# One group of probability transposes, retention scores and value products on TensorE, and a deeper split-ahead for twelve steps

## The chip, the cores and the metric

The kernel runs on one core of one Trainium2 chip. The metric is the time of one execution on the device in microseconds (us), taken as the median of several runs. A difference of under about 0.2% can't be told from no change by this measurement.

## What is computed

One transformer block on 256 tokens of width 1024: a modulation from a conditioning vector, a token mixer with two heads of different kinds (block attention and retention), and a convolutional feed-forward part, each with a layer norm behind it. What matters here is the middle of the mixer. With 256 tokens the attention has a single block, so it is plain causal attention over 8 heads of width 64:

```python
l_own = jnp.einsum('bhqd,bhkd->bhqk', qc, k_own).astype(jnp.float32) * scale
l_own = jnp.where(causal, l_own, NEG_BIG)
...
p = jax.nn.softmax(logits, axis=-1).astype(v.dtype)
...
return (jnp.einsum('bhqk,bhkd->bhqd', p_own, v_own)
...
```

and the retention has 4 heads of key width 128 and value width 256:

```python
scores = jnp.einsum('bhncd,bhnkd->bhnck', qc, kc) * d_intra[None, :, None].astype(dt)
intra = jnp.einsum('bhnck,bhnkv->bhncv', scores, vc)
...
y_r = head_norm(y_r).transpose(0, 2, 1, 3).reshape(b, s, RET_V_W)
y_r = jax.nn.silu(rg) * y_r
merged = jax.nn.sigmoid(g_a) * (y_a @ w_proj_moba) + jax.nn.sigmoid(g_r) * (y_r @ w_proj_ret)
```

The kernel does not scan over chunks: it takes the whole 256 x 256 causal score matrix of a retention head at once and multiplies it by a table of decays.

## The kernel before

**The main stream.** All large products run as *steps*. A weight matrix comes from HBM in raw tiles of 128 x 2048 (1 MB), each of which holds two *halves* of 128 x 1024. A half is split into two fp32r tiles: ScalarE (ACT) copies it to `whi` (L1338) and VectorE (DVE) subtracts that from the raw half to get `wlo` (L1352). A step then multiplies one half on TensorE (PE) with three products, high by high, high by low and low by high (L123 to L125). In the region of this change a step is 12 matmuls of 128x512. There are 4 raw buffers and 8 pairs of split tiles.

**What runs when.** The list `steps` is walked in order. Steps 0 to 7 make the retention's queries and keys, 8 to 11 the second half of its values, 12 to 19 its gate (`winB`, a Silu), 20 to 23 one sigmoid gate (`winGa`), 24 to 31 the other (`winGr`). Products of 12 to 15 go to PSUM banks 2 and 3, of 16 to 19 to 0 and 1, of 20 and 21 to 2 and 3, of 22 and 23 to 0 and 1, and 24 begins with 2 and 3 again. DVE empties the banks of the `winGa` steps (L539) and ACT those of the gate before (L531). In front of each step `prep_to` splits halves ahead: in the range of this change 5 halves beyond that of the step (`NEAR`), as long as fewer than 8 split halves are live. With each half that is split, DVE also gets one product and sum of another part, the modulation (`ada`, L255), as long as such a raw tile is loaded.

**Side work.** Attention and retention are Python generators, advanced at three points of each step: A ahead of the splitting, B behind it, and C behind the step's matmuls. What they issue at C stands on PE behind the matmuls of this step. Every engine takes its own instructions in the order in which they are written. Attention's loop `for i in range(HM + 5)` runs at step 6 + i: its softmax pieces are on ACT at B (L1156, L1160), the reciprocal on DVE at C (L1164). The probabilities of a head, 256 x 256 without the part above the diagonal, are transposed on PE in three blocks of 128x128 into a PSUM bank (L1171) and copied to SBUF by ACT (L1173). That happens behind step 10 for heads 0 and 1, behind step 14 for heads 2 to 5 and behind step 16 for 6 and 7. Behind step 18 stand the attention's value products (`attend`, L1147) and then the retention's scores (L1231), which DVE multiplies by the decay (L1234). Behind step 19 stand the retention's value products (L1219 to L1221), copied out by ACT to `yr` (L1223). All these are plain fp32 matmuls, while the steps are fp32r. The transposes and L1219 to L1221 use the whole array of 128 x 128, L1125 and L1231 two halves of 64 rows, L1147 two halves of 64 columns; so the profile prints 128*128, 64*128 and 128*64.

Of the kernel before, what the change touches and what calls it, by code (L numbers as in the profile page):

```python
# [9 lines left out]
AF = mybir.ActivationFunctionType  # L10
OP = mybir.AluOpType

T, D = 256, 1024
HM, DM = 8, 64
HR, DK, DV = 4, 128, 256
# [2 lines left out]
EPS = 1e-5  # L18
ALPHA = 2.0 ** 0.25
RROPE, RET_AT, TL = 2, 10, 4  # L20
LOOKAHEAD, NEAR, NEAR_TO = 6, 5, 47
RAW_BUFS = 4
HL_BUFS = 8
NG = 4
# [44 lines left out]
def _body(nc, a, out, pe, act, dve, sp, cst, wts, big, tmp, ps, dram):  # L69
    f = lambda ap: ap.bitcast(F32)  # L70

    def bank(i):
        return ps.tile([128, 512], F32, tag=f"P{i}", name=f"P{i}")
# [1017 lines left out]
    def mixers():  # L1091


        qk = S["qk"]
        qkT = [slot(n, [128, 4, 256]) for n in ("3a", "3b")]
        roped = lambda i: rope(qk[i], consts["cosm"][:, i], consts["sinm"][:, i])
        roped(0)
        for i in range(ROT_AT + 2):
            yield
            if i == 1:  # L1100
                roped(1)
            yield
# [12 lines left out]
        blk = [slice(128 * qb, 128 + 256 * qb) for qb in range(2)]  # L1115

        def scores(h):


            S["sc"] = [bank(b) for b in ((4, 7, 5, 6), (2, 3, 4, 7))[h // 4]]  # L1120
            for w in range(2):
                for qb, c in enumerate(blk):
                    for e in range(2):
                        s = slice(64 * e, 64 * e + 64)
                        pe.matmul(S["sc"][2 * w + e][:, c], qkT[0][s, h // 2 + w, qb * 128:(qb + 1) * 128],  # L1125
                                  qkT[1][s, h // 2 + w, :128 + 128 * qb], start=True, stop=True)

        def maxima(h):

            for e in range(2):  # L1130
                sm = S["sms"][:, (h + e) % (TL + 2)]
                mx = tmp.tile([128, 8], F32, name="mx", bufs=TL + 2)
                for qb, c in enumerate(blk):
                    dve.tensor_tensor_reduce(out=sm[:, c], in0=S["sc"][h % 4 + e][:, c],
                                             in1=consts["mask"][:, 128 - 128 * qb:],
                                             scale=-0.125, scalar=3.0e38, op0=OP.add, op1=OP.min,
                                             accum_out=mx[:, 2 + qb:3 + qb])
                st[h + e] = sm, mx

        def attend(h, p):  # L1140

            for w in range(2):
                pT = [pt.pop(h + 2 * w + e) for e in range(2)]
                for kb, (o, c) in enumerate(((slice(0, 256), slice(0, 256)), (slice(128, 256), slice(256, 384)))):
                    for e in range(2):
                        u = h + 2 * w + e
                        pe.matmul(p[64 * e:64 * e + 64, 256 * w + o.start:256 * w + o.stop],  # L1147
                                  v[:, kb, 64 * u:64 * u + 64], pT[e][:, c], start=kb == 0, stop=kb == 1)
            return lambda: split(yah[:, h // 2:h // 2 + 2], yal[:, h // 2:h // 2 + 2], p.rearrange("p (w t) -> p w t", w=2))

        for i in range(HM + 5):
            yield
            if 0 <= i - 2 < HM:
                sm, mx = st[i - 2]
                for qb, c in enumerate(blk):
                    act.activation(sm[:, c], sm[:, c], AF.Copy, scale=mx[:, 6 + qb:7 + qb])  # L1156
            if 0 <= i - 1 < HM:
                sm, mx = st[i - 1]
                for qb, c in enumerate(blk):
                    act.activation(sm[:, c], sm[:, c], AF.Exp, scale=-1.0, bias=mx[:, 2 + qb:3 + qb],  # L1160
                                   accum_out=mx[:, 4 + qb:5 + qb])
            yield
            if 0 <= i - 1 < HM:
                dve.reciprocal(mx[:, 6:8], mx[:, 4:6])  # L1164
            if i == HM + 4:
                done = [attend(4 * g, bank(5 + g)) for g in range(2)]
            for h in {4: (0, 1), 8: (2, 3, 4, 5), 10: (6, 7)}.get(i, ()):
                sm, mx = st.pop(h)
                p = bank(h - 2 if h in (2, 3) else 5 + h % 2)
                for b in range(3):  # L1170
                    pe.transpose(p[:, b * 128:(b + 1) * 128], sm[:, b * 128:(b + 1) * 128], ident)  # L1171
                pT = sm if h > 1 else slot(("9a", "9b")[h], [128, 384])
                act.activation(pT, p[:, :384], AF.Copy)  # L1173
                pt[h] = pT
            if i == 0:
                S["sms"] = slot(11, [128, TL + 2, 384])
            if i in (0, 4):
                scores(i)
            if i in (0, 2, 4, 5):
                maxima(i + i % 2)  # L1180
            if i == RROPE:
                S["turn"] = [rotate(n) for n in range(2)]
            if i >= RROPE and S["turn"] and next(S["turn"][0], 1) == 1:
                S["turn"].pop(0)
            if i == RET_AT:
                sides.append(retention())
            yield
        for fn in done:
            fn()

    def retention():
        rot, decay, sms = S["rot"], S["decay"], S["sms"]
        while S["main"] < RV_AT:
            yield
            yield
            yield
        rv = S["rv"]
        yr = [slot(n, [128, 1024]) for n in ("8a", "8b")]
        SCORES, VALUES = ((4, 7), (2, 3)), (5, 6, 4, 7)
        stt = tmp.tile([128, 8, 6], F32, name="stt", bufs=1)  # L1200
        mv = tmp.tile([128, 8, 2], F32, name="mvr", bufs=1)
        sd = tmp.tile([128, 8], F32, name="sdr", bufs=1)
        ds_ = {}
        for _ in range(3):
            yield
        for n in range(4):
            yield
            if n > 1:
                for t in range(4):
                    g = 2 * n - 4 + t // 2  # L1210
                    dve.bn_stats(stt[:, 2 * g + t % 2], yr[t % 2][:, g * 256:(g + 1) * 256])
                    dve.bn_aggr(mv[:, 2 * g + t % 2], stt[:, 2 * g + t % 2:2 * g + t % 2 + 1])
            yield
            if n == 1:
                for g in range(HR):
                    d_ = ds_.pop(g)
                    p = bank(VALUES[g])
                    c = slice(g * 256, (g + 1) * 256)
                    pe.matmul(p[:, 0:256], d_[:, 0:128], rv[0][:, c], start=True, stop=True)  # L1219
                    pe.matmul(p[:, 256:512], d_[:, 128:256], rv[0][:, c], start=True, stop=False)  # L1220
                    pe.matmul(p[:, 256:512], d_[:, 256:384], rv[1][:, c], start=False, stop=True)  # L1221
                    for t in range(2):
                        act.activation(yr[t][:, c], p[:, t * 256:(t + 1) * 256], AF.Copy)  # L1223
            for m in range(HR // 2 * (n == 0)):
                pp = [bank(b) for b in SCORES[m]]
                for o, ks, qs in ((slice(0, 256), slice(0, 128), slice(0, 256)),
                                  (slice(256, 384), slice(128, 256), slice(128, 256))):
                    for i in range(2):
                        for e, p in enumerate(pp):
                            r_ = slice(64 * e, 64 * e + 64)  # L1230
                            pe.matmul(p[:, o], rot[m][r_, 2 + i, ks], rot[m][r_, i, qs], start=i == 0, stop=i == 1)  # L1231
                for h, p in zip((2 * m, 2 * m + 1), pp):
                    d_ = sms[:, (HM + h) % (TL + 2)]
                    dve.tensor_tensor(d_, p[:, :384], decay[h // 2][:, h % 2], OP.mult)  # L1234
                    ds_[h] = d_
            yield
        S["x"] = [slot(n, [128, 1024]) for n in ("2a", "2b")]
        for i in range(2):
# [148 lines left out]
    for s, (need, rel, fn) in enumerate(steps):  # L1387
        S["main"] = s
        if s == LN1_AT + 8:
            sides.append(residual())  # L1390
        run_sides()
        prep_to(max(need) + 1, True)
        late = LN1_AT < s < LN1_AT + 8
        if not late:
            prep_to(max(need) + 1 + (NEAR if s < NEAR_TO else LOOKAHEAD if s < LN1_AT - 1 else HL_BUFS))
        run_sides()
        for e in waiting:
            if e[0] <= s:
# [120 lines left out]
```

## Time and profile before

| | |
|---|---|
| median of 3 runs | 421.67 us (421.6 to 421.73) |
| the profiled execution's own time | 421.43 us |
| its span in the profile | 419.7 us |
| granted TensorE clock, mean | 0.997 |
| DVE busy from 110 to 118 us | 8.00 of 8.00 us |
| ACT busy from 110 to 118 us | 7.97 of 8.00 us |
| ACT busy from 118 to 124 us | 2.95 of 6.00 us |
| PE busy from 107 to 138 us | 31.00 of 31.00 us |

A page of the profile gives, for one execution, the busy time of each engine, the chain of work that ended last, and the largest groups of instructions. The trace behind it answers closer questions: a timeline by engine, the chain in order of time, who waited for whom. The difference of 1.7 us between own time and span lies around the profiled instructions. Matmuls are pipelined, so the durations of neighbours overlap; the distance from one start to the next tells what one costs.

### The profile page before, as it was taken

To read this page: it belongs to the slowest core of one execution; us is meant where nothing else is said; L and a number is where in the kernel's file an instruction comes from. 1 tells how busy PE (TensorE), PEld (TensorE's weight loads), DVE (VectorE), ACT (ScalarE), POOL (GpSimd) and SP (SyncE) were. 2 spreads that over 40 slices of the span, in tenths; PEclk is the share of its full clock that TensorE was granted. 3 is DMA by queue.
4 is the path that set the end of the run, shared out by engine and by line. 5 is a ranking of instruction groups with operands and counts; after the bars stand their busy time and mean duration, and the time that the engine had idled before them with its cause. 6 is when DMAs were issued, how large, how long until landed. Compare 5 with 4: busy or idle time off the path is not lost.

```text
span 419.7 us, 5879 instructions
## 1 busy us (share of the span) xinstructions
PE 412.5 (98%) x2140; PEld 348.1 (83%) x2140; DVE 368.1 (88%) x597; ACT 248.5 (59%) x410; POOL 14.0 (3%) x26
## 2 busy tenths in 40 slices
PE   7999999999999999999999999999999999999995
PEld 4888888888878888888888898888888888888884
DVE  6889799969998889899887987999999888789996
ACT  5666568787955587535544886555555545455700
POOL 0000000100001000001000001000000010003200
PEclk9999999999999999999999999999999999999998
DMA  8998997685688768789662094985866777450002
GB/s 298 405 410 328 414 404 302 247 324 208 222 308 328 254 244 346 304 319 341 223 269 101 1 361 169 373 295 189 307 260 215 281 284 242 187 198 2 1 6 97
DMA packets 18541, 105.60 MB, mean 252 GB/s; under 512 B 2256, under 2 KB 3536, under 8 KB 7760
## 3 DMA queue, kind: packets, MB, share of 16 engines
q1 hardware_dynamic: 16992, 99.70, 63.1%
q0 software_dynamic: 1376, 4.99, 3.5%
q10 hardware_dynamic: 144, 0.52, 0.5%
q8 instruction: 17, 0.28, 0.3%
q14 instruction: 12, 0.10, 0.1%
HBM read 104.15 MB, written 1.06 MB: 251 GB/s over the span
## 4 chain that ended last, share of the span: by engine, by line
PE 97%; DVE 1%; DMA 1%; issue 0%; DVEq 0%; ACT 0%; ACTq 0%
PE P L134 19%; PE P L123 15%; PE P L124 15%; PE P L125 15%; PE P L329 13%; PE P L138 10%; DMA raw<-in_m 1%; PE P L731 1%; PE P L734 1%; PE P L733 1%; PE P L1125 1%; PE P L1231 1%; PE P L1147 1%; PE P L1171 1%; DVE unread L266 1%; PE P L675 0%
## 5 line engine op out<-in xcount | busy, mean ns | idle before, releaser
L1352 DVE TENSOR_TENSOR wlo<-raw,whi 128x1024 fp32r<-128x1024 f32 x118 | 141.9, 1220 | 14.0 <-ACT whi L1338 13.8
L1338 ACT ACTIVATE whi<-raw 128x1024 fp32r<-128x1024 f32 x118 | 122.1, 1056 | 39.3 <-DMA raw<-in_wpr 10.6
L123 PE MATMUL P<-whi,AH 128*128 128x512 f32 x128 | 50.6, 395 | 0.0
L125 PE MATMUL P<-whi,AH 128*128 128x512 f32 x128 | 49.9, 390 | 0.0
L124 PE MATMUL P<-wlo,AH 128*128 128x512 f32 x128 | 49.8, 389 | 0.0
L329 PE MATMUL P<-whi,AH 128*128 128x512 f32 x160 | 41.7, 391 | 1.1 <-DVE AH L295 1.1
L134 PE MATMUL P<-AYa,whi 128*128 128x512 f32 x144 | 41.7, 391 | 0.0
L255 DVE CUSTOM_DVE_ANT_0 junk<-raw,srow 128x1024 bf16<-128x1024 f32 x32 | 39.0, 1219 | 0.0
L134 PE MATMUL P<-AYb,whi 128*128 128x512 f32 x144 | 38.7, 390 | 0.0
L329 PEld LDWEIGHTS P<-whi,AH 128*128 128x128 f32 x160 | 29.8, 188 | 8.4 <-ACT whi L312 1.9
L489 ACT ACTIVATE A<-P 128x256 f32<-128x256 f32 x36 | 13.7, 381 | 33.9 <-PE P L138 23.6
L134 PEld LDWEIGHTS P<-AYb,whi 128*128 128x128 f32 x144 | 27.0, 188 | 6.0
L312 ACT ACTIVATE whi<-raw 128x512 fp32r<-128x512 f32 (+1 forms) x26 | 20.8, 824 | 17.7 <-DMA raw<-in_b 16.3
L134 PEld LDWEIGHTS P<-AYa,whi 128*128 128x128 f32 x144 | 25.8, 189 | 4.2
L315 DVE TENSOR_TENSOR wlo<-raw,whi 128x512 fp32r<-128x512 f32 (+1 forms) x26 | 23.5, 936 | 6.2 <-ACT whi L312 5.8
L123 PEld LDWEIGHTS P<-whi,AH 128*128 128x128 f32 x128 | 24.0, 188 | 5.2 <-issue 0.3
L125 PEld LDWEIGHTS P<-whi,AH 128*128 128x128 f32 x128 | 24.0, 188 | 5.1
L124 PEld LDWEIGHTS P<-wlo,AH 128*128 128x128 f32 x128 | 24.1, 188 | 4.8
L329 PE MATMUL P<-wlo,AH 128*128 128x512 f32 x80 | 23.2, 390 | 0.0
L138 PE MATMUL P<-AYb,wlo 128*128 128x256 f32 x144 | 23.1, 283 | 0.0
L138 PE MATMUL P<-AYa,wlo 128*128 128x256 f32 x144 | 23.0, 282 | 0.0
L138 PEld LDWEIGHTS P<-AYa,wlo 128*128 128x128 f32 x144 | 20.9, 190 | 1.4
(323 smaller groups left out, 776.1 us busy)
## 6 DMA issues: line engine op xcount, KB each, us to landing
raw<-in_ada SPq DMA_DIRECT2D x16, 1024.0 KB, 5.1
raw<-in_wup SPq DMA_DIRECT2D x11, 1024.0 KB, 5.7
raw<-in_wgate SPq DMA_DIRECT2D x11, 1024.0 KB, 5.7
raw<-in_wdown SPq DMA_DIRECT2D x11, 1024.0 KB, 4.9
raw<-in_winB SPq DMA_DIRECT2D x6, 1024.0 KB, 6.8
raw<-in_m SPq DMA_DIRECT2D x4, 1024.0 KB, 8.3
raw<-in_b SPq DMA_DIRECT2D x4, 1024.0 KB, 7.2
raw<-in_wrot SPq DMA_DIRECT2D x4, 1024.0 KB, 7.4
```

The costliest lines, as they stand in the source:

```text
L123: pe.matmul(o, lh, rh, start=start, stop=False)
L124: pe.matmul(o, lh, rl, start=False, stop=False)
L125: pe.matmul(o, ll, rh, start=False, stop=stop)
L134: pe.matmul(banks()[half], t[0][:, k * 128:(k + 1) * 128], x2(k), start=k == 0, stop=half > 0 and k == 7)
L138: pe.matmul(banks()[half][:, :256], t[1][:, k * 128:(k + 1) * 128], x2(k)[:, 0], start=False, stop=half == 0 and k == 7)
L255: dve.tensor_tensor_reduce(out=nobody(j if own else None), in0=raw, in1=srow, scale=1.0, scalar=0.0, op0=OP.mult, op1=OP.add, accum_out=mo ...
L312: act.activation(hi[:, o], raw[:, o], AF.Copy)
L315: dve.tensor_tensor(lo[:, o], raw[:, o], f(hi[:, o]), OP.subtract)
L329: pe.matmul(pa[b0 + c // 512 * 2 + t], x[xi][:, j, t * 128:(t + 1) * 128], ws[k][:, c:c + 512], start=first and (xi, k) == (0, 0), stop=la ...
L489: act.activation(t, p[:, 256:], AF.Copy)
L1338: act.activation(hi, src, AF.Copy)
L1352: dve.tensor_tensor(lo, src, f(hi), OP.subtract)
```

## The change

The groups of fp32 work behind steps 14, 16, 18 and 19 become one group behind step 17. In it stand, in this order: the transposes of heads 2 to 7, the retention's scores and their decay products, three halves more of splitting (`S["ahead"]`), the attention's value products, the retention's value products and their copies. The decay products are written in place into the decay tile, no longer into the tile of the probabilities. The banks of the group are dealt anew. The splits of the attention's output (`done`) go from the beginning of step 19 to step 18 behind its splitting, and the retention's statistics one step forward. For steps 18 to 29 the splitting is asked to run 8 halves ahead where it ran 5; since a half counts as live until its step is done, that keeps 7 beyond the one in use. The transposes of heads 0 and 1 stay behind step 10.

```diff
-LOOKAHEAD, NEAR, NEAR_TO = 6, 5, 47
+LOOKAHEAD, NEAR, NEAR_TO, WIDE = 6, 5, 47, range(18, 30)
...
+        def turned(hs):
+
+            for h in hs:
+                sm, mx = st.pop(h)
+                p = bank((5, 6, 2, 3, 4, 7, 5, 6)[h])
+                for b in range(3):
+                    pe.transpose(p[:, b * 128:(b + 1) * 128], sm[:, b * 128:(b + 1) * 128], ident)
+                pT = sm if h > 1 else slot(("9a", "9b")[h], [128, 384])
+                act.activation(pT, p[:, :384], AF.Copy)
+                pt[h] = pT
...
-        for i in range(HM + 5):
+        for i in range(HM + 3):
...
-            if i == HM + 4:
-                done = [attend(4 * g, bank(5 + g)) for g in range(2)]
-            for h in {4: (0, 1), 8: (2, 3, 4, 5), 10: (6, 7)}.get(i, ()):
...
+            if i == 4:
+                turned((0, 1))
...
-                sides.append(retention())
-            yield
-        for fn in done:
-            fn()
-
-    def retention():
+                sides.append(retention(lambda: turned(range(2, HM)),
+                                       lambda: [attend(4 * g, bank(5 + g)) for g in range(2)]))
+            yield
+
+    def retention(probs, attend):
...
-        SCORES, VALUES = ((4, 7), (2, 3)), (5, 6, 4, 7)
+        SCORES, VALUES = ((2, 3), (4, 7)), (2, 3, 4, 7)
...
-        for _ in range(3):
-            yield
         for n in range(4):
             yield
+            if n == 1:
+                for fn in done:
+                    fn()
...
+            if n == 0:
+                probs()
+                for m in range(HR // 2):
+                    pp = [bank(b) for b in SCORES[m]]
...
+                    for h, p in zip((2 * m, 2 * m + 1), pp):
+                        d_ = decay[h // 2][:, h % 2]
+                        dve.tensor_tensor(d_, p[:, :384], d_, OP.mult)
+                S["ahead"]()
+                done = attend()
                 for g in range(HR):
-                    d_ = ds_.pop(g)
+                    d_ = decay[g // 2][:, g % 2]
                     p = bank(VALUES[g])
...
+        S["ahead"] = lambda: prep_to(max(need) + 1 + HL_BUFS)
...
-            prep_to(max(need) + 1 + (NEAR if s < NEAR_TO else LOOKAHEAD if s < LN1_AT - 1 else HL_BUFS))
+            prep_to(max(need) + 1 + (HL_BUFS if s in WIDE else NEAR if s < NEAR_TO else LOOKAHEAD if s < LN1_AT - 1 else HL_BUFS))
```

In the changed kernel the lines have other numbers: the transposes are L1146 and their copies L1148, the scores L1225, the decay products L1229, `attend` L1158, the copies to `yr` L1240, the two splits L1345 (`whi`) and L1359 (`wlo`).

The first place is on ACT, between the Silu of the first gate columns (L531, steps 12 to 15) and the copies of the transposed probabilities. Before (`P` is a PSUM bank, `A_848` the tile of the probabilities, DMAHW6 and DMAHW0 are the loads of two raw tiles):

```order
L531 ACTIVATE A7b<-P_1051 128x512 [waits PE_49]
L1338 ACTIVATE whi<-raw 128x1024 [waits DMAHW6_49]
L1173 ACTIVATE A_848<-P_1186 128x384 [waits PE_49]
L1173 ACTIVATE A_848<-P_1191 128x384 [waits PE_49,Activation_49]
L1338 ACTIVATE whi<-raw 128x1024
L1338 ACTIVATE whi<-raw 128x1024 [waits DMAHW0_49]
```

Of the change, from the same Silu on:

```order
L531 ACTIVATE A7b<-P_1051 128x512 [waits PE_49]
L1345 ACTIVATE whi<-raw 128x1024 [waits DMAHW6_49]
L1345 ACTIVATE whi<-raw 128x1024
L1148 ACTIVATE A_848<-P_1192 128x384 [waits PE_49]
L1148 ACTIVATE A_848<-P_1197 128x384 [waits PE_49]
L1148 ACTIVATE A_848<-P_1202 128x384 [waits PE_49]
```

Four of the copies stood ahead of this Silu before; now all six stand behind both halves of the raw tile that DMAHW6 brings, and ahead of the tile of DMAHW0.

The second place is on DVE, from the decay products to the splits of the attention's output (L101, into `A_812`). Before, with one half (L1352) and one modulation product (L255) in front of it:

```order
L1352 TENSOR_TENSOR wlo<-raw,whi 128x1024
L255 ISA junk,mod<-raw,srow 128x1024
L255 ISA mod 128x1
L1234 TENSOR_TENSOR A_848<-P_1260,A2a 128x384
L1234 TENSOR_TENSOR A_848<-P_1261,A2a 128x384
L1234 TENSOR_TENSOR A_848<-P_1272,A2b 128x384
L1234 TENSOR_TENSOR A_848<-P_1273,A2b 128x384
L101 TENSOR_TENSOR A_812<-P_1242,A_811 128x512
```

Of the change, from the last decay product on:

```order
L1229 TENSOR_TENSOR A2b<-P_1235,A2b 128x384
L1359 TENSOR_TENSOR wlo<-raw,whi 128x1024
L255 ISA junk,mod<-raw,srow 128x1024
L255 ISA mod 128x1
L1359 TENSOR_TENSOR wlo<-raw,whi 128x1024
L255 ISA junk,mod<-raw,srow 128x1024
L255 ISA mod 128x1
L1359 TENSOR_TENSOR wlo<-raw,whi 128x1024
L101 TENSOR_TENSOR A_812<-P_1266,A_811 128x512
```

One half and its modulation product went from ahead of the decay products to behind them, and two halves and one more modulation product came in ahead of the splits.

More of the change, by code (lines that the diff above doesn't have):

```diff
@@ L1164, in mixers @@
                 dve.reciprocal(mx[:, 6:8], mx[:, 4:6])
-            if i == HM + 4:
-                done = [attend(4 * g, bank(5 + g)) for g in range(2)]
-            for h in {4: (0, 1), 8: (2, 3, 4, 5), 10: (6, 7)}.get(i, ()):
[L1168 to L1174, printed above, removed]
+            if i == 4:
+                turned((0, 1))
             if i == 0:
@@ L1185, in mixers @@
             if i == RET_AT:
-                sides.append(retention())
+                sides.append(retention(lambda: turned(range(2, HM)),
+                                       lambda: [attend(4 * g, bank(5 + g)) for g in range(2)]))
             yield
-        for fn in done:
-            fn()
-    def retention():
-        rot, decay, sms = S["rot"], S["decay"], S["sms"]
+    def retention(probs, attend):
+        rot, decay = S["rot"], S["decay"]
         while S["main"] < RV_AT:
@@ L1202, in retention @@
         sd = tmp.tile([128, 8], F32, name="sdr", bufs=1)
-        ds_ = {}
-        for _ in range(3):
-            yield
         for n in range(4):
             yield
+            if n == 1:
+                for fn in done:
+                    fn()
             if n > 1:
@@ L1213, in retention @@
             yield
-            if n == 1:
+            if n == 0:
+                probs()
+                for m in range(HR // 2):
+                    pp = [bank(b) for b in SCORES[m]]
+                    for o, ks, qs in ((slice(0, 256), slice(0, 128), slice(0, 256)),
+                                      (slice(256, 384), slice(128, 256), slice(128, 256))):
+                        for i in range(2):
+                            for e, p in enumerate(pp):
+                                r_ = slice(64 * e, 64 * e + 64)
+                                pe.matmul(p[:, o], rot[m][r_, 2 + i, ks], rot[m][r_, i, qs], start=i == 0,
+                                          stop=i == 1)
+                    for h, p in zip((2 * m, 2 * m + 1), pp):
[3 more added lines that the diff above has]
+                done = attend()
                 for g in range(HR):
-                    d_ = ds_.pop(g)
+                    d_ = decay[g // 2][:, g % 2]
                     p = bank(VALUES[g])
@@ L1223, in retention @@
                         act.activation(yr[t][:, c], p[:, t * 256:(t + 1) * 256], AF.Copy)
[L1224 to L1235, printed above, removed]
+            yield
+        for _ in range(3):
             yield
```

## Prediction

> **What bounds the kernel now.** I read the page first: shares, granted clock and chain.
>
> ```profile
> span 419.7 us, 5879 instructions
> PE 412.5 (98%) x2140; PEld 348.1 (83%) x2140; DVE 368.1 (88%) x597; ACT 248.5 (59%) x410; POOL 14.0 (3%) x26
> PEclk9999999999999999999999999999999999999998
> PE 97%; DVE 1%; DMA 1%; issue 0%; DVEq 0%; ACT 0%; ACTq 0%
> ```
>
> The reader is to see that PE is busy nearly throughout, at full granted clock, and that the chain is PE. A busy PE is not yet a PE that loses nothing, so I went on to the chain in order of time between 110 and 138 us, where all that is moved lies. Its columns are start, length and line; there the lengths are distances, not overlapping durations.
>
> ```profile
> 110.32 1.31 PE P L1171 x12
> 111.63 0.23 PE P L123
> ...
> 117.12 0.65 PE P L1171 x6
> 117.78 0.23 PE P L123
> ...
> 123.23 2.75 PE P L1147 x32
> 125.99 2.82 PE P L1231 x32
> 128.80 0.43 PE P L123
> ...
> 136.50 0.43 PE P L1221 x2
> 136.94 0.23 PE P L123
> ```
>
> A matmul of the main stream costs 0.227 us (0.23 here). From 117.78 to 123.23 stand the 24 of steps 17 and 18: 5.45 / 24 = 0.227. No step waits for a half here, so **splitting further ahead has no PE wait to remove**. What can be gained is what the fp32 groups cost beyond their own work. A transpose costs 1.31 / 12 = 0.109, and the first matmul behind both groups of transposes takes its plain 0.23: going into and out of transposes is free. So are the value products, 0.43 a pair with 0.23 behind. The two groups between are not. Their pairs, once running, go like this:
>
> ```profile
> 123.43 0.38 PE L1147 MATMUL P<-A9a,A 128*64 128x256 f32 x1
> 123.65 0.27 PE L1147 MATMUL P<-A9a,A 128*64 128x128 f32 x1
> 123.76 0.27 PE L1147 MATMUL P<-A9a,A 128*64 128x128 f32 x1
> ```
>
> The starts are 0.22 apart behind a pair of 256 columns and 0.11 behind one of 128. Either group has 8 pairs of each, so (0.216 + 0.109) x 8 = 2.60. L1147 took 2.75 (0.15 over), L1231 2.82 (0.22 over), and the first fp32r matmul behind 0.43 in place of 0.23 (0.20 over): **0.57 us for three changes of the array's shape**. With the stretches of main matmuls behind the groups, of which that from 111.63 to 117.12 (24 in 5.49) lost 0.05, all four groups lose some 0.65 us, 0.15% of the kernel. That is the most that merging them could bring.
>
> **The change part by part.**
>
> *Shapes.* The group goes from the main stream into transposes (free), to L1225 in two halves of rows, to L1158 in two halves of columns, to the value products on the whole array, and back (free). That is again three changes. Neither rows to columns nor columns to whole is in the trace. The nearest rows are the three above, 0.15 to 0.22 each, and the round trip of attention's scores, whole to rows and back:
>
> ```profile
> 97.70 1.51 PE P L1125 x16
> 99.21 0.43 PE P L123
> ```
>
> Its 4 pairs of each size are 1.30; 1.51 + 0.43 - 1.30 - 0.23 = 0.41 for two changes. So the third costs between nothing (then 0.41 in all, 0.16 less than now) and, as dear as the dearest, 0.22 and a bit (0.63 in all, 0.06 more). I take 0.57, the same as now, as 0.15 to 0.22 apiece is what every change in these rows cost. What goes is the 0.05 to 0.10 of small losses behind three groups. **Term: -0.07 us, between -0.25 and +0.05.**
>
> [...]
>
> *The group's inner waits.* This is where the change can lose. Everything in the group used to be made ready by ACT one or more steps before PE came back for it; now PE comes back at once. PE arrives early: the first group is gone, so steps 15 to 17 run from 110.32 for 36 x 0.227 = 8.16 to 118.48. The 18 transposes take 18 x 0.109 = 1.96, to 120.44 (120.3 to 120.4 by starts, which run 0.1 ahead of this chain). Then L1225 writes banks 2 and 3, which hold the transposed heads 2 and 3 until ACT has copied them. Where is ACT? Before:
>
> ```profile
> 112.66 1.59 ACT L1173 ACTIVATE A<-P 128x384 f32<-128x384 f32 x4
> ...
> 115.09 0.80 ACT L1156 ACTIVATE A<-A,mx 128x128 f32<-128x128 f32 x2
> 115.91 1.28 ACT L531 ACT_TABLE_LOAD   x1
> 117.20 0.60 ACT L531 ACTIVATE A7a<-P 128x512 f32<-128x512 f32 x1
> ...
> 118.18 1.06 ACT L1338 ACTIVATE whi<-raw 128x1024 fp32r<-128x1024 f32 x1
> 119.15 0.85 ACT L1173 ACTIVATE A<-P 128x384 f32<-128x384 f32 x2
> ...
> 126.58 1.06 ACT L1338 ACTIVATE whi<-raw 128x1024 fp32r<-128x1024 f32 x1 [5.64 <-DMA raw<-in_winGr]
> ```
>
> Four copies (1.59) go away ahead of the Silu. That does not bring all of it forward: L1156 waits for DVE's reciprocal, and the next `whi` for its raw tile. The first row here is of the table of busy time by stretch (PE, weight loads, DVE, ACT, POOL, clock, DMA): DVE has no gap from 110 to 118 us. The last is of the list of transfers, from issue to landing.
>
> ```profile
> 110.00:118.00 8.00, 8.00 (x46) 6.83 (x45) 8.00 (x13) 7.97 (x19) 0.00 (x0) 1.00 0.67 255
> ...
> 114.24 0.17 DVE L1164 RECIPROCAL mx<-mx 128x2 f32<-128x2 f32 x1
> ...
> 113.24 0.33 SPq L110 DMA_DIRECT2D raw<-in_winGa  x1
> ...
> raw<-in_winGa SPq DMA_DIRECT2D x1, 1024.0 KB, 4.9
> ```
>
> From 114.4 on L1156 (0.8), table load (1.28) and Silu (0.98, from 117.20 to 118.18) end at about 117.5, 0.7 sooner than now. The raw tile was issued at 113.24, when DVE freed its buffer, and lands 4.9 later at 118.15. DVE's order up to there is the same, so the landing stays. `whi` starts at about 118.18 as before. In the changed order its second half follows before any copy: one `whi` starts 0.97 behind the other (118.18 to 119.15), so the copies begin at 118.18 + 1.94 = 120.12. Their distance is (1.59 - 0.48) / 3 = 0.37, where 0.48 is one alone (0.85 - 0.37). Head 2 is out at 120.6, head 3 at 120.97. The scores' matmuls come in pairs, one to each bank, so the first pair is whole at 121.0 instead of 120.4. **Term: +0.6 us.** It would be zero if the tile landed 0.6 sooner. Of loads of this size
>
> ```profile
> DMA to landing us min/median/max: 4.7/4.8/4.9
> ...
> DMA to landing us min/median/max: 4.8/6.5/7.5
> ```
>
> the two of `in_winGa` took 4.7 to 4.9, those of `in_winGr` up to 7.5. Bounds: 0 and 2.6 + 0.6 = 3.2; I take 0.6, as it is this very load that has to be waited for, and its own row says 4.9.
>
> Nothing else in the group should wait. The second pair of heads needs banks 4 and 7, copied by 121.7, at 121.0 + 1.4 = 122.4. `attend` begins at about 123.8 and needs all copies (122.5). The tile of DMAHW0, for which ACT stood 5.64 us, now stands behind the copies. DVE reaches the decay products when it has done what is ahead of them:
>
> ```profile
> 123.69 1.22 DVE L1352 TENSOR_TENSOR wlo<-raw,whi 128x1024 fp32r<-128x1024 f32 x1
> 124.83 1.22 DVE L255 CUSTOM_DVE_ANT_0 junk<-raw,srow 128x1024 bf16<-128x1024 f32 x1
> 127.52 1.02 DVE L1234 TENSOR_TENSOR A<-P,A2a 128x384 f32<-128x384 f32 x2 [1.47 <-PE P L1231]
> ...
> 129.77 1.28 DVE L101 TENSOR_TENSOR A<-P,A 128x512 fp32r<-128x512 f32 x2
> ```
>
> The half at 123.69 now stands behind them, so they run from 123.7 to 125.7 (1.02 a pair), while the value products begin at 123.8 + 2.75 + 0.2 = 126.7. That cover is 2.5 us for the first head, 1.4 for the last pair at the least.
>
> *Splitting ahead.* Three more halves, with two or three modulation products, at 1.14 apiece (123.69 to 124.83), are the same work earlier. Halves are made some five steps before use, so this costs PE nothing unless it delays something that PE waits for. That is L539, which empties banks 2 and 3 for step 24:
>
> ```profile
> 143.03 1.26 DVE L539 TENSOR_TENSOR A<-P,A 128x512 f32<-128x512 f32 x2
> 133.37 0.38 ACT L1223 ACTIVATE A8b<-P 128x256 f32<-128x256 f32 x1
> 135.53 0.42 DVE L1211 BATCH_NORM_STATS2 stt<-A8a 128x6 f32<-128x256 f32 x1
> 137.57 0.18 DVE L1212 BATCH_NORM_AGGREGATE mvr<-stt 128x2 f32<-128x6 f32 x1
> ```
>
> From 125.7 the new order has on DVE up to L539: six halves and five modulation products (11 x 1.14 = 12.5), the splits L101 (1.2) and two blocks of statistics (2.1 each, 135.53 to 137.65): 18.0, to 143.7. To that come waits for ACT: L101 needs L100, which stands behind eight copies to `yr`; the last of these follows the last value product at about 132, and ACT is through with L100 at 133.9, where DVE could start at 131.4. With 0.4 more behind it, L539 runs at about 146.5 and has the first bank free at 147.1. PE begins step 24 with six steps of 2.72 behind the group's end at 131.8: 148.1. The cover is 1.0 us; it was about 3.9 (143.65 against 136.94 + 10.9 less the 0.3 of the chain). **Term: 0.** POOL's loads of x now wait for the value products instead of the decay products; x is first read behind step 47, and SP's later loads are each needed several steps on.
>
> *Sum.* -0.07 + 0.6 = **+0.5 us**. The profiled execution took 421.43 (1.7 outside its span of 419.7), so it would take 421.95. The median of the runs before is 421.67, 0.24 higher, and the forecast for the median is 421.67 + 0.55 = **422.2 us**, 0.13% more. A measurement of this kernel tells about 0.2% (0.84 us) from no change, so this counts as the same.
>
> **The rivals.**
>
> *Enough cover.* The copies come in time, because the tile lands sooner or the Silu frees ACT early enough for a different meeting. Then only -0.07 is left, 421.6 (421.4 to 421.7). For it speaks that 0.6 us is little beside the spread of loads of this size (4.7 to 7.5); against it that DVE, which sets the issue, has no slack before. Chance 0.21.
>
> *DVE late at step 24.* If DVE falls over 1.0 us further behind between the decay products and L539, PE waits for bank 2, one for one. DVE is the engine with least room (8.00 of 8.00 us from 110 to 118), and each further wait for ACT or for a load moves all behind it. At 1 us beyond the point it gives 422.2 + 1.0 = 423.2, slower. Against it: DVE's idle stretches are counted in already, and the 1.47 in a row above is gone. Chance 0.14.
>
> *A slower clock.* The group begins with 1.96 us of transposes and a wait of 0.6, and TensorE's clock might be taken down for it. If the scores behind ran at half rate, 2.82 more: 425.0, slower. Against it: the row of the granted clock shows 9 through every group, and behind the 12 transposes at 110.32 the next matmul took 0.23 and the stretch's clock is 1.00. Chance 0.03. [...]
>
> *The change brings more than these rows hold.* Faster by over 0.84 us needs a loss that the chain doesn't show, as the whole of it here is 0.65. At 1 us it gives 420.7. Chance 0.06.
>
> **How the numbers follow.** The forecast has 0.56; of this 0.06 lies above 422.5, where the wait grows over 0.9. So *slower* is 0.06 + 0.14 + 0.03 = 0.23, *faster* 0.06, and *same* 0.50 + 0.21 = 0.71. The range goes from 421.3 (all saved at the lower bound of the shapes, no wait: 421.67 - 0.25 and the spread of the runs) to 423.2 (DVE late by 1 us). Left out are the clock, the rest of the late landings and a larger gain.
>
> **What would show it.** Step by step: the chain behind step 17 shows the transposes at 0.109 and then the first of L1225 some 0.6 late, with ACT's copies as releaser; L1225, L1158 and the value products follow with 0.15 to 0.25 over their own length each and no wait; ACT has two `whi` between Silu and copies, the first at about 118.2; L539 runs near 146 and step 24 starts unhindered. It is wrong if L1225 starts at once, if PE waits for the decay products or at step 24, or if the clock falls below 9.

## Result and profile after

The changed kernel takes **423.93 us** (median of 7 runs, 423.65 to 426.26). Beside it the kernel before took 421.64 us (421.38 to 421.77, 7 runs). The ratio is 1.0065, with a 95% interval of 1.0054 to 1.0075: slower by 0.65%, 2.3 us. The forecast was 422.2, and the range up to 423.2 does not hold the result.

The profiled execution is the slowest of the seven (426.26 us own time, span 424.5), so it shows more than the median does. Four lines of its page answer to those of before:

```profile
span 424.5 us, 5881 instructions
PE 415.0 (98%) x2140; PEld 349.9 (82%) x2140; DVE 368.4 (87%) x597; ACT 248.9 (59%) x410; POOL 14.0 (3%) x26
PEclk9999999999999999989999999999999999999999
PE 73%; DVE 11%; DMA 8%; ACT 5%; issue 2%; DVEq 0%; ACTq 0%; SPq 0%
```

The busy shares of the engines hardly moved, and PE is still busy 98% of the span. What changed is the chain: PE's share fell from 97% to 73%, and DVE, DMA and ACT took the rest. Somewhere PE is now led by others. The clock's row has one 8, the 18th of 40 slices of 10.6 us, from 180.4 to 191.0 us.

First the group itself. From the timeline of after (start, length, engine, line; in brackets the idle time ahead and its releaser), on PE and ACT:

```profile
118.62 2.13 PE L1146 MATMUL P<-ident,A 128*128 128x128 f32 x18
121.13 1.13 PE L1225 MATMUL P<-AR 64*128 64x256 f32 x6 [0.39 <-ACT A L1148]
118.69 2.01 ACT L1345 ACTIVATE whi<-raw 128x1024 fp32r<-128x1024 f32 x2 [0.53 <-DMA raw<-in_winGa]
120.60 2.38 ACT L1148 ACTIVATE A<-P 128x384 f32<-128x384 f32 x6
```

PE ends its 18 transposes at 118.62 + 18 x 0.109 = 120.58 and starts the scores at 121.13, 0.55 us later, for the copies, which stand behind two `whi`, the first of which waited for its load. That is the forecast wait, in its forecast place. Behind it the chain of after in order of time (start, length) shows the rest of the group:

```profile
121.13 3.26 PE P L1225 x26
124.39 2.75 PE P L1158 x32
127.14 0.63 PE P L1236 x2
127.77 0.43 PE P L1237 x2
...
132.52 0.23 PE P L123
```

A part of the wait lies inside the scores: they take 3.26 us here and 2.82 where nothing holds them, since the second bank waits for the copy of its own head. By the timeline, 3.74 us pass from the end of the transposes (120.58) to the first of L1158 (124.32), and 2.91 in the kernel "not wide, heads early" of the experiments, whose group has no such wait. So the copies cost 0.83 us in all in this execution. The value products follow without a wait.

The large loss comes over 60 us later. From the timeline of after, first around L539, then at step 36, the first product of the retention's projection (`AYa` holds the retention's normalised output):

```profile
147.51 1.28 DVE L539 TENSOR_TENSOR A<-P,A 128x512 f32<-128x512 f32 x2
148.28 1.28 ACT L540 ACT_TABLE_LOAD   x1 [6.46 <-DVE A L539]
150.63 1.04 ACT L1345 ACTIVATE whi<-raw 128x1024 fp32r<-128x1024 f32 x1
151.71 1.23 DVE L1359 TENSOR_TENSOR wlo<-raw,whi 128x1024 fp32r<-128x1024 f32 x1 [2.91 <-ACT whi L1345]
...
184.29 1.28 DVE L554 TENSOR_TENSOR A<-P,A 128x512 f32<-128x512 f32 x2
185.12 0.47 PE L123 MATMUL P<-whi,AYa 128*128 128x512 f32 x1 [1.83 <-DVE A L554]
186.17 0.63 PE L123 MATMUL P<-whi,AYa 128*128 128x512 f32 x1
```

Step 24 starts without a wait, since L539 is in time. But PE stands before step 36, from 183.1 to 185.1: **2.0 us**. Its banks 2 and 3 have to be emptied by L554, DVE's sum of the attention's projection. Then seven matmuls follow each other at 0.427 instead of 0.227 us (the chain shows 0.43), and those around them are partly slow, 1.7 us more in this execution. That is the 8 in the clock's row.

The same place before, from its timeline on SP, ACT, DVE and PE:

```profile
167.24 0.33 SPq L110 DMA_DIRECT2D raw<-in_wpr  x1
172.15 1.06 ACT L1338 ACTIVATE whi<-raw 128x1024 fp32r<-128x1024 f32 x1 [1.93 <-DMA raw<-in_wpr]
173.11 1.06 ACT L100 ACTIVATE AYa<-P 128x512 fp32r<-128x512 f32 x2
178.40 1.29 DVE L554 TENSOR_TENSOR A<-P,A 128x512 f32<-128x512 f32 x2
182.08 0.39 PE L123 MATMUL P<-whi,AYa 128*128 128x512 f32 x1
```

PE can start 0.83 us behind the start of L554 (184.29 to 185.12), and there were 3.68: a cover of 2.85 us. Now L554 starts 5.89 later, and PE would have come 1.05 later: 5.89 - 1.05 - 2.85 = 1.99, the wait. The chain of after in order of time tells where the 5.9 come from:

```profile
157.43 0.61 DVE A L539
...
158.07 0.65 ACT A L540 x2
...
159.20 1.05 ACT whi L1345
...
160.28 1.24 DVE wlo L1359
...
161.53 4.78 DMA raw<-in_wpm
...
166.42 1.06 ACT whi L1345
...
170.23 1.24 DVE wlo L1359
171.47 0.02 issue
171.48 6.46 DMA raw<-in_wpr
...
178.03 1.06 ACT whi L1345
179.09 0.50 ACT AYa L100
...
179.61 1.29 DVE AYa L101 x2
180.90 1.15 DVE AYb L101 x2
...
184.37 0.61 DVE A L554
```

One chain of four engines, none of them full. A `wlo` on DVE frees a raw buffer, SP issues the next load into it, ACT makes `whi` of that load, and behind this `whi` in ACT's order stand the copies L100 of the retention's output, which DVE needs for L101, behind which stands L554. The load of `in_wpr` was issued at 171.48, 4.24 later than before, and took 6.46 us, 1.6 more than before (4.82, from 167.24 to 172.07). Both count: by subtraction, a load of 4.82 would have left 0.35 of the wait of 1.99.

Why is the chain late if the splitting was asked to run further ahead? The busy time from 148 to 160 us, before and then after (columns: us, PE, weight loads, DVE, ACT, POOL, clock, DMA share, GB/s):

```profile
148.00:160.00 12.00, 12.00 (x55) 9.93 (x54) 11.15 (x20) 9.45 (x15) 0.00 (x0) 1.00 0.68 240
```

```profile
148.00:160.00 12.00, 12.00 (x54) 9.93 (x54) 7.65 (x13) 9.13 (x11) 0.00 (x0) 1.00 0.53 207
```

DVE works 3.5 us less there. The rows around L539 above say why: the extra halves stand on DVE ahead of L539, which so starts at 147.51, 4.5 us later than the 143.03 of before. ACT's L540 waits 6.46 us for it. The next `whi` stands behind L540 in ACT's order and is done at 151.7, and until then DVE has nothing left to split: it idles 2.91 us right behind L539. What was done early is missing later, and DVE, ACT and the loads hand the delay on to each other to step 36.

### The profile page after: what moved, and what is told of

Its sections match the earlier page's. It is cut to its first block, busy times and chain, and to the rows that moved or that the text cites. A ratio compares the mean times of both kernels' runs of the same rounds, so it can differ in the third digit from the quotient of the medians.

```text
span 424.5 us, 5881 instructions
## 1 busy us (share of the span) xinstructions
PE 415.0 (98%) x2140; PEld 349.9 (82%) x2140; DVE 368.4 (87%) x597; ACT 248.9 (59%) x410; POOL 14.0 (3%) x26
## 4 chain that ended last, share of the span: by engine, by line
PE 73%; DVE 11%; DMA 8%; ACT 5%; issue 2%; DVEq 0%; ACTq 0%; SPq 0%
PE P L134 18%; PE P L329 11%; PE P L123 9%; PE P L125 9%; PE P L124 9%; PE P L138 9%; DVE wlo L1359 3%; ACT whi L1345 2%; DVE junk L255 2%; DMA raw<-in_winB 2%; DMA raw<-in_b 2%; DMA raw<-in_wpr 2%; DMA raw<-in_winGa 1%; DMA raw<-in_wpm 1%; DMA raw<-in_m 1%
## 5 line engine op out<-in xcount | busy, mean ns | idle before, releaser
L1359 DVE TENSOR_TENSOR wlo<-raw,whi 128x1024 fp32r<-128x1024 f32 x118 | 142.0, 1220 | 19.5 <-ACT whi L1345 19.0
L1345 ACT ACTIVATE whi<-raw 128x1024 fp32r<-128x1024 f32 x118 | 122.2, 1058 | 41.0 <-DMA raw<-in_wpr 12.8
L255 DVE CUSTOM_DVE_ANT_0 junk<-raw,srow 128x1024 bf16<-128x1024 f32 x32 | 39.0, 1219 | 0.0
```

The lines of the kernel that those rows point to most:

```text
L255: dve.tensor_tensor_reduce(out=nobody(j if own else None), in0=raw, in1=srow, scale=1.0, scalar=0.0, op0=OP.mult, op1=OP.add, accum_out=mo ...
L1345: act.activation(hi, src, AF.Copy)
L1359: dve.tensor_tensor(lo, src, f(hi), OP.subtract)
```

## Experiments

Each ran beside the kernel before on the same chip, so that the ratios are within one comparison. L554 and the waits are of one profiled execution each; the wait at step 36 is what the distance between two starts of matmuls there has above 0.227. A ratio with its interval is taken over the runs of a comparison and need not be the quotient of two medians.

| kernel | median us (lowest to highest) | ratio, 95% | L554 starts | PE waits at step 36 |
|---|---|---|---|---|
| change, again | 423.18 (422.75–423.83) | 1.0037 [1.0025, 1.0049] | 183.54 | 1.92 |
| group only | 422.81 (422.32–426.23) | 1.0032 [1.0021, 1.0044] | 184.26 | 2.73 |
| wide steps only | 425.33 (424.79–428.25) | 1.0105 [1.0081, 1.013] | 185.03 | 1.23 |
| change, not ahead inside | 426.28 (425.78–427.26) | 1.0116 [1.01, 1.0131] | 185.51 | 0.25 |
| change, not wide | 422.10 (421.79–422.49) | 1.0009 [1.0001, 1.0018] | 178.64 | 0 |
| change, wide to step 46 | 428.78 (427.82–430.92) | 1.0176 [1.0152, 1.0199] | 186.98 | 3.99 |
| change, retention split first | 421.96 (421.61–422.85) | 1.0009 [1.0, 1.0018] | 179.95 | 0 |
| change, 6 ahead instead of 8 | 422.05 (421.66–423.79) | 1.0017 [1.0008, 1.0026] | 181.04 | 0 |
| change, heads early | 422.05 (421.65–423.71) | 1.002 [1.001, 1.003] | 181.40 | 0.28 |
| change, both repairs | 421.51 (421.21–421.68) | 0.9999 [0.999, 1.0008] | 179.60 | 0 |
| not wide, heads early | 421.68 (421.24–422.11) | 1.0001 [0.9992, 1.001] | 179.32 | 0 |
| the same, retention split first | 421.48 (421.35–421.74) | 0.9999 [0.9991, 1.0008] | 177.63 | 0 |

In the six of these executions with a wait at step 36, and in the change's first, PE starts step 36 at 0.83 or 0.84 us behind the start of L554, whatever releaser the trace names there. Without a wait the distance is longer.

**The change again.** No edit.

> The changed kernel unchanged, for a second profile. Both theories: about 423.9 us. The first profile holds a wait of 2.0 us at step 36 (the first product of the retention's projection) and behind it eight matmuls at 0.427 us instead of 0.227. The mean clock of the other executions is 0.997 to 1.000, so a second profile should show the wait of about 2 us and the inner wait of the group of 0.55 us, and not the eight slow matmuls.

423.18 us, 0.75 less than in the first comparison. The wait at step 36 is there (1.92), and the matmuls behind it run at full clock (1.00 from 184 to 190 us). The chain of the group:

```profile
118.63 1.97 PE P L1146 x18
120.60 3.16 PE P L1225 x26
```

Here the scores start at once behind the transposes, and the whole inner wait lies between the two banks: 3.16 less 2.82 is 0.34 us. So both waits belong to the change, the inner one with a size that differs from execution to execution, and the slow matmuls of the first profile belong only to some executions.

**The group without any deeper splitting.**

```diff
-LOOKAHEAD, NEAR, NEAR_TO, WIDE = 6, 5, 47, range(18, 30)
+LOOKAHEAD, NEAR, NEAR_TO, WIDE = 6, 5, 47, ()
...
-        S["ahead"] = lambda: prep_to(max(need) + 1 + HL_BUFS)
+        S["ahead"] = lambda: None
```

> The change with both parts of the deeper splitting taken out: the one group behind step 17 stays, no three halves in it, 5 halves ahead throughout. Theory DEPTH (the deeper splitting sets DVE and ACT back against each other, so that the load of the retention's projection comes late and with it the emptying of bank 2, L554, for step 36): no wait at step 36, the inner wait of 0.55 us stays, 422.1 to 422.3 us. Rival GROUP (the group alone puts DVE back by its inner order, the depth is innocent): the wait at step 36 stays, 423.3 us or more.

422.81 us, between the two expectations and so a miss of both, spread from 422.32 to 426.23; the profiled execution is the slowest and waits 2.73 us at step 36 (its load of `in_wpr` ran from 170.46 to 177.93). In its timeline of DVE:

```profile
133.92 1.29 DVE L101 TENSOR_TENSOR A<-P,A 128x512 fp32r<-128x512 f32 x2 [6.10 <-ACT A L100]
```

DVE has no half to split ahead of L101 and idles 6.10 us, until ACT's copies L100, which stand behind all copies of the group. So the group alone, with nothing ahead in it, makes the chain late enough to reach step 36 in some executions.

**The deeper splitting without the group**, in the kernel before.

```diff
-LOOKAHEAD, NEAR, NEAR_TO = 6, 5, 47
+LOOKAHEAD, NEAR, NEAR_TO, WIDE = 6, 5, 47, range(18, 30)
...
-            prep_to(max(need) + 1 + (NEAR if s < NEAR_TO else LOOKAHEAD if s < LN1_AT - 1 else HL_BUFS))
+            prep_to(max(need) + 1 + (HL_BUFS if s in WIDE else NEAR if s < NEAR_TO else LOOKAHEAD if s < LN1_AT - 1 else HL_BUFS))
```

> The kernel before with the deeper splitting alone: 8 halves ahead in steps 18 to 29, the four fp32 groups where they were. Theory DEPTH: no inner wait in a group, but L554 late and a wait of 1 to 2 us at step 36, 422.7 to 423.7 us. Rival GROUP: no wait, 421.6 to 421.8 us.

425.33 us, above both expectations. There are three waits, and theory DEPTH had excluded the first, which is inside a group: 1.94 before the retention's value products (L1219, whose decay products come late on DVE), 0.47 at step 24 (L539), 1.23 at step 36. Splitting ahead without the group costs more than with it: in the old order DVE gets the extra halves ahead of the decay products, which run from 130.81 to 132.67, behind two halves more than before (split at 127.39 and 129.68).

**The group and the three halves inside it, no wide steps.**

```diff
-LOOKAHEAD, NEAR, NEAR_TO, WIDE = 6, 5, 47, range(18, 30)
+LOOKAHEAD, NEAR, NEAR_TO, WIDE = 6, 5, 47, ()
```

> The change with the three halves in the group kept and the depth of steps 18 to 29 back at 5. Theory DEPTH in the form that the running at the limit of 8 live tiles does the harm: no wait at step 36, 422.1 to 422.4 us. If the three halves in the group do it: a wait at step 36 as in the change, 423.3 us or more. Rival GROUP: 423.3 us or more as well; with the group alone beside it the two are told apart.

422.10 us, no wait at step 36, L554 back at 178.64. L539 starts at 141.62, and the load of `in_wpr` is issued at 167.50, where it was 171.48 and 170.76 in the change; DVE is busy 12.00 of the 12 us from 148 to 160. What is left is the wait in the group (0.47 us by the measure used above). DVE's idle time ahead of L101 is 1.76 us instead of the 6.10 of the group alone: the three halves inside the group fill that hole. So **the wide steps make the wait at step 36** of the change, and the three halves, without them, prevent what the group alone would do.

**The group and the wide steps without the halves inside the group.**

```diff
-        S["ahead"] = lambda: prep_to(max(need) + 1 + HL_BUFS)
+        S["ahead"] = lambda: None
```

> The change without the three halves in the group; steps 18 to 29 still ask for 8. If the running at the limit of 8 live tiles does the harm (theory DEPTH, as the run without it at 422.1 us says): the wait at step 36 is there, 422.8 to 423.5 us. If it takes both: 422.1 us.

426.28 us: missed. In its timeline (DVE, then PE) the rival of the prediction appears:

```profile
133.49 1.22 DVE L1359 TENSOR_TENSOR wlo<-raw,whi 128x1024 fp32r<-128x1024 f32 x1 [5.72 <-ACT whi L1345]
149.20 1.28 DVE L539 TENSOR_TENSOR A<-P,A 128x512 f32<-128x512 f32 x2
149.94 0.50 PE L123 MATMUL P<-whi,AH 128*128 128x512 f32 x1 [1.80 <-DVE A L539]
150.61 0.63 PE L125 MATMUL P<-whi,AH 128*128 128x512 f32 x1
```

The hole is back (5.72 us), and the wide steps' halves are made behind it, ahead of L539. That comes at 149.20 instead of 147.51, and PE waits 1.96 us for it at step 24, with slow matmuls behind. By step 36 PE itself comes so late that only 0.25 is left to wait.

**Wide to step 46.** This asks whether the splitting starves behind step 29, where the demand drops back from 8 to 5.

```diff
-LOOKAHEAD, NEAR, NEAR_TO, WIDE = 6, 5, 47, range(18, 30)
+LOOKAHEAD, NEAR, NEAR_TO, WIDE = 6, 5, 47, range(18, 47)
```

> The change with the depth of 8 kept on until step 46 instead of step 29. If the harm is done in steps 18 to 29, where ACT's splitting waits behind the two sigmoids (L540) and these for DVE's L539: as the change or a little less, 422.8 to 423.3 us. If it is the pause of two steps behind step 29, in which no half is split and no load is started: no wait at step 36, 422.1 us.

428.78 us: missed, in the other direction. PE waits 1.17 at 176.85 (on ACT's L547) and 3.99 at step 36. The drop at step 29 is not the cause; it is what limits the damage.

**The retention split first.** The whole change, but the copies and splits of the retention's output (L100, L101) are written two calls earlier, ahead of step 32's products and of the `whi` for which ACT waited.

```diff
-        for _ in range(11):
+        for _ in range(9):
```

> The change with the transposes and splits of the retention's output one step's length earlier (in front of step 32's products, not behind them), so that on ACT their copies (L100) stand ahead of the half of the retention's projection that waits for its load. Depth and group are as in the change. Theory CHAIN (step 36 waits for bank 2, emptied by L554, which stands on DVE behind the splits L101, which stand behind that load on ACT): L554 at about 181.5 us instead of 183.5 to 184.3, ahead of step 36; the wait of 1.9 us goes and the inner one of 0.55 stays: 421.9 to 422.3 us. Rival: the wait at step 36 is for the split halves themselves, which this edit doesn't bring forward: 423.2 us as the change.

421.96 us. From its timeline, ACT and DVE:

```profile
171.33 1.10 ACT L100 ACTIVATE AYa<-P 128x512 fp32r<-128x512 f32 x2
176.30 2.01 ACT L1345 ACTIVATE whi<-raw 128x1024 fp32r<-128x1024 f32 x2 [1.95 <-DMA raw<-in_wpr]
179.95 1.28 DVE L554 TENSOR_TENSOR A<-P,A 128x512 f32<-128x512 f32 x2
```

The load is issued as late as in the change again (170.82 against 170.76), but L100 no longer stands behind it, L554 starts at 179.95, and PE has no wait at step 36. In this execution the load also lands 1.0 us sooner (176.2 against 177.2). In the old order L554 stood 6.33 behind that landing (177.21 to 183.54); that would have put it at 182.55, from where PE needs 0.83, and PE, which starts step 36 at 182.43, would still have waited 0.95 us. One link cut out of the chain takes away the wait, with the late splitting untouched, and the highest of eleven runs is 422.85. That shows the link: it is the order on ACT, late `whi` ahead of L100, through which the deeper splitting reaches PE.

**Six halves ahead instead of eight.**

```diff
-            prep_to(max(need) + 1 + (HL_BUFS if s in WIDE else NEAR if s < NEAR_TO else LOOKAHEAD if s < LN1_AT - 1 else HL_BUFS))
+            prep_to(max(need) + 1 + (LOOKAHEAD if s in WIDE else NEAR if s < NEAR_TO else LOOKAHEAD if s < LN1_AT - 1 else HL_BUFS))
```

> Between: the twelve steps are asked for 6 halves ahead instead of 8 (the group keeps its three halves ahead). Theory of the chain (the deeper the demand, the more raw tiles, halves and modulation products stand ahead of the retention's splits, and the later L554 empties banks 2 and 3 for step 36): L554 between the 178.6 of the kernel without the wide steps and the 184.3 of the change, near 181; PE needs it at about 183, so no wait or under 0.5 us there, and 422.1 to 422.6 us in all. Rival (it is not depth but that something ahead of the group is asked for earlier at all): 423.2 as the change, with a wait of about 2 us at step 36.

422.05 us with L554 at 181.04 and no wait at step 36: as the theory of the chain had it, with a time 0.05 us under its range. Single executions reach 423.79. Asked for 5, 6 and 8 halves, L554 starts at 178.64, 181.04 and 183.54 to 184.29. This kernel also shows that a late L539 is not enough by itself. It starts at 146.16, close to the 146.85 of the change again, but DVE's next `wlo` follows without a gap at 147.36, because its `whi` was made ahead of L540, and the load is issued at 169.25 and not at 170.76.

**Heads early.** Heads 2 to 5 are transposed and copied behind step 14 again, 6 and 7 in the group. This is to take away the wait in the group, as banks and copies are then free when the scores start.

```diff
-                p = bank((5, 6, 2, 3, 4, 7, 5, 6)[h])
+                p = bank((5, 6, 0, 1, 5, 6, 5, 6)[h])
...
-            if i == 4:
-                turned((0, 1))
+            if i in (4, 8):
+                turned((0, 1) if i == 4 else (2, 3, 4, 5))
...
-                sides.append(retention(lambda: turned(range(2, HM)),
+                sides.append(retention(lambda: turned((6, 7)),
```

First without the wide steps:

> The change with the depth of steps 18 to 29 back at 5 (422.1 us) and, beside that, the transposes of heads 2 to 5 back behind step 14, so that banks 2 and 3 need no copy before the retention's scores. If the inner wait is what is left of the loss, as forecast: the first of L1225 follows the transposes at once, 0.55 us less, 421.5 to 421.7 us, the same as before. If merging gains something by itself that the waits hid: under 421.3 us.

421.68 us, 0.42 less than without this edit, and the same as before. The chain of this kernel in order of time:

```profile
119.85 0.66 PE P L1146 x6
120.51 2.82 PE P L1225 x32
123.33 2.75 PE P L1158 x32
126.08 0.63 PE P L1236 x2
126.71 0.43 PE P L1237 x2
```

Here the group runs without a wait, and the price of the shapes can be read: L1225 2.82 and L1158 2.75 over a plain 2.60, and the first pair of the value products 0.63 instead of 0.43: 0.22 + 0.15 + 0.20 = 0.57 us.

Then the same with the wide steps:

> The change with heads 2 to 5 transposed and copied behind step 14 again and nothing else: the fourth cell beside the change (423.2 to 423.9), the change with earlier splits of the retention (421.96) and the change with both (421.51). If the two waits are separate and add up, the wait in the group is worth what it was worth between the last two, 0.45 us, and this kernel takes 422.7 to 423.4 us, with a wait of 1.5 to 2 us at step 36 and none in the group. Rival (the wait in the group is what makes DVE late at step 36, since DVE's decay products and the copies on ACT stand behind it): no wait at step 36 either, and 421.5 to 421.9.

422.05 us: between the two expectations, and so a miss of both. PE still waits at step 36, but only 0.28 us. In its timeline (SP issues the load, ACT uses it):

```profile
170.29 0.33 SPq L110 DMA_DIRECT2D raw<-in_wpr  x1
175.15 1.06 ACT L1345 ACTIVATE whi<-raw 128x1024 fp32r<-128x1024 f32 x1 [3.27 <-DMA raw<-in_wpr]
```

The load was issued 0.47 earlier than in the change again (170.76), about what PE itself is ahead (0.5), but landed at 175.1, 4.8 us behind the issue instead of 6.4. That makes up the rest of the difference at step 36, and 0.28 is about what the change's first execution would have waited with a load of that length (0.35). The profiled execution is the fastest of twelve (421.65); the others reach up to 423.71. So the late issue uses up the cover, and how long PE then waits depends on the load. How long this load takes from one execution to the next was not settled.

**Both repairs**: the edits of "retention split first" and "heads early" together in the full change, with wide steps and halves inside.

> The change with both repairs: heads 2 to 5 transposed and copied behind step 14 again (only 6 and 7 in the group), and the retention's splits two calls earlier, ahead of step 32's products. Wide steps and the halves ahead inside the group stay. If the two waits (0.55 us in the group, about 2 us at step 36) are all that the change costs: 421.5 to 421.7 us, the same as before, with no PE wait over 0.1 us between 110 and 190. If the deep splitting costs something else that the trace of the change does not show as a wait: over 422.0.

421.51 us beside 421.55 of before, no wait from 110 to 190 us. The two waits are all that the change costs, as far as can be measured.

**No wide steps, heads early, retention split first.**

> As the kernel with heads 2 to 5 early and no wide steps (421.68, equal to before), with the retention's splits earlier as well. PE waits nowhere between 110 and 190 in either, so earlier splits have nothing to remove: 421.5 to 421.8 us, ratio to before 0.9995 to 1.0005. A rival by which slack at step 36 is worth something by itself would give under 421.3.

421.48 us: slack at step 36 is worth nothing in itself. No version is faster than the kernel before by an amount that can be measured.

## Why the prediction was wrong

**Where it failed: the term 0 of splitting ahead.** The prediction put it so: the extra halves are "the same work earlier", which "costs PE nothing unless it delays something that PE waits for. That is L539, which empties banks 2 and 3 for step 24". The condition was right, the list behind it too short. It named one user of DVE's results, at the next place where PE needs a bank, and stopped there. L539 is also what ACT waits for (L540), and `whi` stands behind L540; so a late L539 stops the splitting itself once DVE has used up the halves whose `whi` was made ahead of L540. "SP's later loads are each needed several steps on" was true of the halves in the loads, and not of L100, which stands behind such a load's `whi` on ACT and was not looked for. In place of the 0 the runs showed a chain of late L539, late `whi`, late load, late L100 and late L554, which ends in a wait of 1.9 to 2.0 us at step 36. The medians put 1.1 to 1.8 us there (423.18 or 423.93, less the 422.10 without wide steps), or 1.2 to 2.0 less the 421.96 with the retention split first. How much of it is the load's varying length stays open.

**PE is the bound, and no step waits for a half; merging can bring 0.65 us at most.** Right. With both waits repaired, which needs the transposes of heads 2 to 5 back behind step 14, the kernel with the rest in one group is as fast as before (0.9999, 0.999 to 1.0008).

**Shapes, -0.07 us.** Right within what can be told: three changes at 0.22, 0.15 and 0.20, 0.57 as taken. The two that no row had shown, rows to columns (0.15) and columns to whole (0.20), cost what the others do. Merging groups that differ in shape saved nothing here: three changes and 0.57 us before, three changes and 0.57 us with the group (not wide, heads early).

**The group's inner wait, +0.6 us.** Right in place, releaser and, roughly, size: two `whi` between Silu and copies, the first at 118.69 (118.2 forecast), 0.83 us in the first profile, 0.34 in the second, and 0.42 and 0.45 us by the medians when it is taken away. The prediction was to be wrong if L1225 started at once. In the second profile it did, and the wait lay between the two banks, so that sign was too narrow. Nothing else in the group waited; the decay products ran from 124.2 to 126.2 and the value products began at 127.1.

**L539 near 146, step 24 unhindered.** It came at 147.51 and 146.85. PE could have started 0.74 behind it (149.20 to 149.94 in the kernel that waits), at 148.25, and it came to step 24 at 148.72. The cover was 0.5 us in the first profile, and held. The forecast had 1.0.

**The rival of DVE late at step 24** named the right engine and the wrong step. It happens, with 1.96 us, in the kernel without the halves inside the group. In the change the same lateness of DVE is handed on, through ACT's order and a load, to step 36. The delay, 4.5 us at L539, had grown to 5.9 at L554.

**Enough cover, and a slower clock.** The copies did not come in time for both banks, so the first did not happen. The clock did fall, but not in the group: behind 1.96 us of transposes and a wait of 0.55 it stayed at 1.00 (121.2 to 133 us), and it fell to 0.50 behind the wait at step 36 (from 185.55 us).

With the two terms as measured, the sum would have been 421.67 + 0.45 - 0.07 + 1.1 to 1.8, or 423.2 to 423.9. That it meets the result confirms nothing, since the last term was taken from the change's own times.

## What to carry to other kernels

Work done earlier on an engine with little slack was paid here by what stood there, L539 on DVE, 4.5 us later. Follow such an instruction to all its readers, on the other engines too, and ask what stands behind each of them in order, until the chain ends in slack. A deeper look-ahead with the same number of raw buffers did not load sooner here (`in_wpr` was issued 4.24 us later); it moved the splits in front of results that the next splits had to wait for. If a late load cannot be avoided, see that nothing urgent stands behind its first user; here two calls in the order were worth the whole wait at step 36.

## What the hardware showed beside that

Behind a wait of PE of about 2 us the clock was halved in some executions and not in others. Behind 1.96 us (no halves inside) and 1.99 (change) seven matmuls came at 0.427 us in place of 0.227, and behind 2.73 (group only) and 3.99 (wide to step 46) they came at 0.43 as well; behind 1.92 (change again) they came at 0.227 but for the first, and behind 1.94 (wide steps only) the granted clock is 1.00 (128 to 138 us). The table of busy time by stretch gives the clock as 0.50 from 185.55 to 188.96 us in the change, and as 1.00 on both sides. That is 3.41 us. With no halves inside it gives 0.79 from 146 to 154 us, and in the group only 0.72 from 184 to 190; split into 0.50 and 1.00 that is an estimated 3.4 us at 0.50 in each. In wide to step 46 it gives 0.55 from 186 to 192 us, an estimated 5.4 us at 0.50, and the chain has nine matmuls at 0.43 us from 188.58 us on. Why the clock was halved behind 1.96 us and not behind 1.94 was not settled.

The same 1 MB load of `in_wpr` took 4.8 us (before), 5.4 (retention split first), 6.4 (change again) and 7.5 (group only). Times spread wide where the chain to PE runs through this load with no slack, 422.3 to 426.2 us for the group alone against 421.2 to 421.7 with both repairs. Where L100 stands behind the load with slack to spare (change, not wide), they run from 421.8 to 422.5. How much of the spread is the load's was not measured.
